# A hybrid attention block's first stage: scaling x in advance on POOL and DVE, both parts of u from ACT, weight loads on POOL's queue, fewer matrix-vector streams on TensorE

## The chip, the core and the metric

The kernel runs on one core of a Trainium2 chip. Its time is the device time of one execution in microseconds (us); a lower one is better. The engines are named as in the profile: PE (TensorE), DVE (VectorE), ACT (ScalarE), POOL (GpSimd) and SP (SyncE), which here only issues DMAs.

## The reference, cut to what matters

One decoder block over 512 tokens of width 2048, all in float32. The part that the first stage computes:

```
mod = silu(c) @ w_ada + b_ada                 # w_ada: 2048 x 12288; sections sh1, sc1, g1, sh2, sc2, g2
u   = rmsnorm(x, norm_attn) * (1 + sc1) + sh1
z   = u @ w_in                                # 2048 x 5664
...                                           # two kinds of attention on the columns of z, output product,
                                              # gated residual, SwiGLU, final RMSNorm
```

Of `mod`, only the sections sh1 and sc1 are needed for u: two matrix-vector products with 2048 x 2048 weights each.

## The kernel before, in words

**Layout.** Everything is kept transposed: a tile has 128 features on the partitions and the 512 tokens in a row. x is loaded by token and turned by PE into `xT` (16 tiles), and the row `rstd1` (1/rms of every token, the same on all partitions) comes from the sums of squares. A product in near float32 precision is made of three fp32r matmuls, for which each operand is split into a high part h (rounded by ACT) and a low part l (the rest, by DVE). So u is 16 pairs (h, l), and a `unit` is the three matmuls of one weight block with one u pair. Weights are loaded (`fetch_w`, tile `wr`), split by ACT into `wh` (L244) and by DVE into `wl` (L249).

**The first stage** is one loop over `step`, with its order written out by hand (`manual_schedule`): the instructions of each engine run in the order in which the loop emits them, and engines wait for each other by data alone. There are 8 rounds of 8 steps. Step n loads tile `ad` n: 256 rows of w_ada for 256 columns of sc1 and 256 of sh1, two DMAs on SP's queue (L509) into a ring of 8. A round is thus the mod values for two blocks of 128 features, and so for two tiles of u. In detail:

- One step after its load, DVE multiplies tile n by the entries of silu(c) and adds it to `acc` (L531, L533): a tile has two 128-row halves, one operation each. Where `on_pe(n)` is true, the second half is given to PE one step later, as a matmul with the broadcast column of silu(c) (L540, called a stream below), and gathered in a PSUM row that ACT copies out (`row`, L544).
- After the round's last tile, PE sums `row` and `acc` over the partitions by eight small matmuls each (L552); DVE adds the bias (`mod`, L560), forms `a_vec` = (1 + sc1) * norm_attn (L400), and `modulate_a` makes `mt` = xT * a_vec * rstd1 on DVE (L414) and h = round(mt + sh1) on ACT (L416). A step later `modulate_b` makes l = (mt + sh1) - h on DVE (L420).
- With two more tiles of u, units become possible. They wait in the list `todo` and are popped into PE's order at each step. Four PSUM banks `S0` gather the first half of the query product over u 0 to 7 (copied out by `keep_half`) and then the product `p_cmp` over all of u; three banks `S1` gather `p_s1` over all of u.
- `w_pairs(j)` asks for the weights of a round at step 8j+2 (round 0: at step 7) on SP's queue, in tiles shared by three or two buffers. In rounds 5 to 7 there are three of them, and the third is split at the round's fourth step, after the `modulate_a` of the third. Up to round 4 there are two, split at the round's first two steps.
- `tables()` builds the sine and cosine tables of the rotary embedding, one DVE operation a step, from step 14 on.

After the loop SP stores xT to DRAM (`xsp`, L590) behind the three weight loads of the next GEMM; memory of the stage is then used by the rotary steps (L609 to L616), which free the banks `S1` for that GEMM (second half of the query product).

Of the kernel before, what the change touches and what calls it, by code (L numbers as in the profile page):

```python
# [27 lines left out]
LAG = 2  # L28
LAGS = 2, 3, 4, 6
LAGS0 = 1, 2, 3, 0  # L30
KEEP = 12
R_C, R_D, R_F, R_V = 1.0, 1.0, 1.0, 0.6
SCALE = HD ** -0.5
NCMP = 31
# [45 lines left out]
def hymba_block(ctx: ExitStack, tc: tile.TileContext, x, c, positions, w_ada, b_ada, norm_attn,  # L80
# [21 lines left out]
    def uid(s):  # L102
        n_uid[0] += 1
        return f"{s}_{n_uid[0]}"
# [112 lines left out]
    def load_w(parts, ct, nk=2, extra=None, src=None, width=T, bufs=3):  # L217
        return fetch_w(parts, ct, nk, extra, src, width, bufs)()

    def fetch_w(parts, ct, nk=2, extra=None, src=None, width=T, bufs=3):  # L220
        pl = src or wts
        wr = pl.tile([P, nk, width], F32, tag="wr", name=uid("wr"), bufs=bufs)
        w = 0
        for part, n in parts:
            nc.sync.dma_start(wr[:, :, w:w + n], part(ct * nk * P, nk))
            w += n

        held = []

        def high():  # L230
            n_split[0] += 1
            if spare and n_split[0] % 3 == 0:
                both = spare[0].tile([P, 2, nk, width], F32R, tag="wx", name=uid("wx"), bufs=1)
                wh, wl = both[:, 0], both[:, 1]
            else:
                wh = pl.tile([P, nk, width], F32R, tag="wh", name=uid("wh"), bufs=2)
                wl = pl.tile([P, nk, width], F32R, tag="wl", name=uid("wl"), bufs=2)
            todo = [(slice(0, w), wr[:, :, 0:w])]
            if extra is not None:
                e = extra[:, ct * nk:(ct + 1) * nk, :]  # L240
                todo.append((slice(w, w + e.shape[2]), e))
            held.extend((wh, wl, todo))
            for sc, v in todo:
                nc.scalar.copy(wh[:, :, sc], v)  # L244
                if not early_high:
                    low(sc, v)

        def low(sc, v):
            nc.vector.tensor_tensor(held[1][:, :, sc], v, split_ap(held[0])[:, :, sc], op=OP.subtract)  # L249

        early_high = []

        def halves():
            if not held:
                high()
            else:
                for sc, v in held[2]:
                    low(sc, v)
            return held[0], held[1]

        def high_now():
            early_high.append(1)
            high()

        halves.high = high_now
        return halves
# [136 lines left out]
    def act_tile(name, i):  # L403
        h = act.tile([P, T], F32R, tag="ah", name=uid(name + "h"), bufs=ND)
        l = act.tile([P, T], F32R, tag="al", name=uid(name + "l"), bufs=ND)
        return h, l

    def modulate(which, i, src, rb, pl):
        return modulate_b(*modulate_a(which, i, src, rb, pl))

    def modulate_a(which, i, src, rb, pl):
        sh = mod[:, (0 if which == 0 else 3) * ND + i:(0 if which == 0 else 3) * ND + i + 1]
        t = pl.tile([P, T], F32, tag="mt", name=uid("mt"), bufs=2)
        nc.vector.scalar_tensor_tensor(t, src, a_vec[:, which, i:i + 1], rb, op0=OP.mult, op1=OP.mult)  # L414
        h, l = act_tile("u", i)
        nc.scalar.activation(h, t, AF.Identity, bias=sh)  # L416
        return h, l, t, sh

    def modulate_b(h, l, t, sh):
        nc.vector.scalar_tensor_tensor(l, t, sh, split_ap(h), op0=OP.add, op1=OP.subtract)  # L420
        return h, l

    cosT = sinT = None

# [32 lines left out]
    p_cmp = [cols(w_in, C_KC, 512)]  # L457
    p_s1 = [cols(w_in, C_KS, 256), cols(w_in, C_KW, 128)]
    part = None
    u = []  # L460
    NJ = ND // 2
    HJ = NJ // 2

    def w_pairs(j):
        s1 = fetch_w(p_s1, j, src=early, width=3 * P, bufs=2)
        if j < HJ:
            return [fetch_w(p_qn, j), s1]
        i = 2 * (j - HJ)
        return [fetch_w(p_cmp, i), s1, fetch_w(p_cmp, i + 1)]

    def unit(w, k, i, n, m, outs):
        return lambda: bank_pieces(("ws", m * P, P, outs[m]))[0](w[0], w[1], k, u[i], i == 0, i == n - 1)
# [21 lines left out]

    def on_pe(n):
        j, r = divmod(n, 8)
        return r < 7 if j == 0 else 2 <= r < (6 if j <= HJ else 4)

    tiles, accs, rows, sums, halves, fetched, todo = {}, {}, {}, {}, {}, {}, []
    extra_work = tables()  # L500
# [2 lines left out]
    while step < SLOTS + 8 or todo:  # L503
        j, r = divmod(step, 8)
        if j < NJ:
            tiles[step] = early.tile([P, 2, T], F32, tag="adw", name=uid("ad"), bufs=ADW)
            for i, sec in ((0, 1), (1, 0)):
                c0 = sec * D + j * 256
                nc.sync.dma_start(tiles[step][:, :, i * 256:(i + 1) * 256],  # L509
                                  w_ada[:, c0:c0 + 256].rearrange("(q p) n -> p q n", p=P)[:, 2 * r:2 * r + 2, :])  # L510
        if r == (2 if j else 7) and j < NJ:
            fetched[j] = w_pairs(j)
        if j == 1 and r < 2:
            fetched[0][r].high()
        i = AT.get(r, 3) if j < NJ else AT_END.get(r, 3)
        if 1 < j <= NJ and i < len(fetched[j - 1]):
            w = fetched[j - 1][i]()
            halves.setdefault(j - 1, []).append(w)
            pr = 2 * (j - 1 - HJ) + i // 2
            if j > HJ and i != 1:  # L520
                todo += units(w, pr, S0, ND)
        n = step - 1
        if 0 <= n < SLOTS:
            jj, q0 = n // 8, 2 * (n % 8)
            if q0 == 0:
                accs[jj] = early.tile([P, T], F32, tag="acc", name=uid("acc"), bufs=2)
            acc = accs[jj]
            for q in range(1 if on_pe(n) else 2):
                sc1 = sl[:, q0 + q:q0 + q + 1]
                if q0 + q == 0:  # L530
                    nc.vector.tensor_scalar(acc, tiles[n][:, q, :], sc1, None, op0=OP.mult)  # L531
                else:
                    nc.vector.scalar_tensor_tensor(acc, tiles[n][:, q, :], sc1, acc, op0=OP.mult, op1=OP.add)  # L533
        n = step - 2
        if 0 <= n < SLOTS and on_pe(n):
            jj, q = n // 8, 2 * (n % 8) + 1
            first = n == 0 or not on_pe(n - 1)
            if first:
                rows[jj] = bank("mm")
            nc.tensor.matmul(rows[jj], sl[:, q:q + 1].to_broadcast([P, P]), tiles[n][:, 1, :],  # L540
                             start=first, stop=not on_pe(n + 1))
            if not on_pe(n + 1):
                row = early.tile([1, T], F32, tag="row", name=uid("row"), bufs=2)
                nc.scalar.copy(row, rows[jj][0:1, :])  # L544
                rows[jj] = row
        n = due(step, 0)
        if n is not None:
            jj = n // 8
            sums[jj] = bank("mm")
            for av, one in ((rows.pop(jj), one_col[0:1, :]), (accs.pop(jj), one_col)):  # L550
                for i in range(4):
                    nc.tensor.matmul(sums[jj][:, i:i + 1], av[:, i * P:(i + 1) * P], one,  # L552
                                     start=one is not one_col and i == 0, stop=one is one_col,
                                     skip_group_check=True)
        n = due(step, 1)
        if n is not None:
            jj = n // 8
            for k2, sec in ((0, 1), (1, 0)):
                m0 = sec * ND + 2 * jj
                nc.vector.tensor_tensor(mod[:, m0:m0 + 2], sums[jj][:, 2 * k2:2 * k2 + 2], b_mod[:, m0:m0 + 2],  # L560
                                        op=OP.add)
            scale_vec(0, jj * 2, 2)
            pend = [modulate_a(0, i, xT[:, i, :], rstd1, early) for i in (2 * jj, 2 * jj + 1)]
            if jj == 0:
                halves[0] = [fetched[0][0]()]
        n = due(step, 2)
        if n is not None:
            u.extend([modulate_b(*h) for h in pend])
            jj = n // 8
            if jj == 0:  # L570
                halves[0].append(fetched[0][1]())
            if jj < HJ:
                todo += units(halves[jj][0], jj, S0, ND // 2) + units(halves[jj][1], jj, S1, ND)
            if jj == HJ - 1:
                todo.append(keep_half)
        n = due(step, 3 if step < SLOTS else 2)
        if n is not None and n // 8 >= HJ:
            todo += units(halves[n // 8][1], n // 8, S1, ND)
        for _ in range(3 if step >= 8 * HJ + LAGS[3] else 1 + (len(todo) > KEEP)):
            if todo:  # L580
                todo.pop(0)()
        if step >= 14:
            next(extra_work, None)
        step += 1
        if step == SLOTS + 6:
            z_first = [fetch_w(p_qn, HJ + i) for i in range(3)]
            w = z_first[0]()
            z_first[0] = lambda w=w: w
# [838 lines left out]
```

## Time and profile before

| | |
|---|---|
| median of 3 runs | 2457.55 us (2456.65 to 2460.13) |
| the profiled execution | 2450.92 us, of which the span of the trace is 2448.0 us |
| PE busy | 2355.1 us (96%) |
| PE weight loads busy | 2100.4 us (86%) |
| DVE busy | 1579.6 us (65%) |
| ACT busy | 1016.0 us (42%) |
| POOL busy | 341.5 us (14%) |
| mean granted clock of PE | 0.981 |

The span is the time from the first to the last instruction of one execution; windows are counted in us from its start. Busy times of different engines overlap. A granted clock of 1.00 is PE's higher level (2.4 GHz), 0.50 the lower one (1.2 GHz); a figure between them is a mean over a stretch that had both.

### The profile page before, as it was taken

To read this page: it belongs to the slowest core of one execution; us is meant where nothing else is said; L and a number is where in the kernel's file an instruction comes from. 1 tells how busy PE (TensorE), PEld (TensorE's weight loads), DVE (VectorE), ACT (ScalarE), POOL (GpSimd) and SP (SyncE) were. 2 spreads that over 40 slices of the span, in tenths; PEclk is the share of its full clock that TensorE was granted. 3 is DMA by queue.
4 is the path that set the end of the run, shared out by engine and by line. 5 is a ranking of instruction groups with operands and counts; after the bars stand their busy time and mean duration, and the time that the engine had idled before them with its cause. 6 is when DMAs were issued, how large, how long until landed. Compare 5 with 4: busy or idle time off the path is not lost.

```text
span 2448.0 us, 38482 instructions
## 1 busy us (share of the span) xinstructions
PE 2355.1 (96%) x14717; PEld 2100.4 (86%) x14717; DVE 1579.6 (65%) x2711; ACT 1016.0 (42%) x1531; POOL 341.5 (14%) x370
## 2 busy tenths in 40 slices
PE   6998999999999989889999999999999999999998
PEld 4677887888888767789999999999999888888887
DVE  6876786887755576596777777777776643333333
ACT  3224544344423332365555555555555422222133
POOL 0003002000001121251222121212221100000010
PEclk8998999999999999999999999999999999999999
DMA  9864743463554277559898989898988644333322
GB/s 332 283 198 147 205 139 95 130 190 117 180 174 129 85 249 253 186 122 237 211 231 215 228 213 232 220 225 212 221 200 193 192 151 141 123 120 121 102 95 101
DMA packets 322713, 440.31 MB, mean 180 GB/s; under 512 B 26224, under 2 KB 217552, under 8 KB 322528
## 3 DMA queue, kind: packets, MB, share of 16 engines
q1 hardware_dynamic: 289104, 348.21, 44.0%
q0 software_dynamic: 31120, 85.45, 18.7%
q10 hardware_dynamic: 2304, 4.20, 0.5%
q8 instruction: 115, 1.88, 0.3%
q14 instruction: 70, 0.57, 0.1%
HBM read 340.18 MB, written 28.38 MB: 151 GB/s over the span
## 4 chain that ended last, share of the span: by engine, by line
PE 54%; DVE 1%; DMA 0%; issue 0%; ACT 0%; SPq 0%; DVEq 0%; ACTq 0%
PE py L1161 12%; PE py L1164 11%; PE py L1163 11%; PE psmm L278 3%; PE psmm L279 3%; PE psmm L280 3%; PE pss L278 2%; PE pss L279 2%; PE pss L280 2%; PE pso L279 1%; PE pso L278 1%; PE pso L280 1%; DMA wr<-in_w_down_dram 0%; PE pso L1058 0%; DVE ul L1141 0%
## 5 line engine op out<-in xcount | busy, mean ns | idle before, releaser
L249 DVE TENSOR_TENSOR wl<-wr,wh 128x1024 fp32r<-128x1024 f32 (+2 forms) x211 | 239.0, 1133 | 381.5 <-ACT wh L244 378.4
L244 ACT CAST wh<-wr 128x1024 fp32r<-128x1024 f32 (+2 forms) x211 | 199.5, 948 | 502.7 <-PE psmm L279 199.7
L1164 PE MATMUL py<-uh,ls 128*128 128x256 f32 x1408 | 397.6, 282 | 3.6 <-DVE ls L1107 3.6
L1163 PE MATMUL py<-ul,hs 128*128 128x256 f32 x1408 | 397.6, 282 | 2.2 <-DVE ul L1141 2.2
L1161 PE MATMUL py<-uh,hs 128*128 128x256 f32 x1408 | 398.4, 283 | 1.0 <-DVE ev L1178 0.5
L1107 DVE TENSOR_TENSOR ls<-sum,hs 128x1024 fp32r<-128x1024 f32 x176 | 215.2, 1223 | 196.5 <-ACT hs L1101 196.5
L1101 ACT CAST hs<-sum 128x1024 fp32r<-128x1024 f32 x176 | 184.5, 1049 | 377.3 <-PE py L1163 257.5
L1163 PE MATMUL py<-ul,hx 128*128 128x256 f32 x1056 | 298.8, 283 | 4.0 <-DVE ul L1141 4.0
L1161 PE MATMUL py<-uh,hx 128*128 128x256 f32 x1056 | 299.3, 283 | 1.7 <-ACT uh L1140 1.4
L1164 PE MATMUL py<-uh,lx 128*128 128x256 f32 x1056 | 298.3, 282 | 0.0
L1164 PEld LDWEIGHTS py<-uh,ls 128*128 128x128 f32 x1408 | 267.0, 190 | 4.7 <-DVE ls L1107 4.6
L1163 PEld LDWEIGHTS py<-ul,hs 128*128 128x128 f32 x1408 | 267.0, 190 | 3.3 <-DVE ul L1141 3.3
L1161 PEld LDWEIGHTS py<-uh,hs 128*128 128x128 f32 x1408 | 267.1, 190 | 2.7 <-DVE ev L1178 1.3
L1097 POOL DMA_DIRECT2D lx<-raw x176 | 156.2, 887 | 580.2 <-ACT lx L1096 419.4
L1163 PEld LDWEIGHTS py<-ul,hx 128*128 128x128 f32 x1056 | 200.8, 190 | 5.1 <-DVE ul L1141 5.1
L1161 PEld LDWEIGHTS py<-uh,hx 128*128 128x128 f32 x1056 | 200.6, 190 | 2.2 <-ACT uh L1140 1.7
L1164 PEld LDWEIGHTS py<-uh,lx 128*128 128x128 f32 x1056 | 200.7, 190 | 0.0
L386 DVE SCALAR_TENSOR_TENSOR acc<-ad,sl,acc 128x512 f32<-128x512 f32 x180 | 141.6, 787 | 43.2 <-DMA ad<-in_w_ada_dram 41.4
L1092 ACT CAST hx<-raw 128x768 fp32r<-128x768 f32 x176 | 144.3, 820 | 11.3 <-DMA raw<-in_w_gate_dram 11.3
L1096 ACT ACTIVATE lx<-raw 128x768 fp32r<-128x768 f32 x176 | 148.1, 841 | 1.8 <-DMA raw<-in_w_gate_dram 1.8
L278 PE MATMUL psmm<-fh,wh 128*128 128x512 f32 x352 | 137.0, 389 | 0.0
L280 PE MATMUL psmm<-fh,wl 128*128 128x512 f32 x352 | 136.9, 389 | 0.0
(441 smaller groups left out, 5284.3 us busy)
## 6 DMA issues: line engine op xcount, KB each, us to landing
lx<-raw POOLq DMA_DIRECT2D x176, 384.0 KB, 5.2
ad<-in_w_ada_dram SPq DMA_DIRECT2D x128, 512.0 KB, 4.1
raw<-in_w_up_dram SPq DMA_DIRECT2D x176, 256.0 KB, 4.2
raw<-in_w_gate_dram SPq DMA_DIRECT2D x176, 256.0 KB, 4.5
wr<-in_w_down_dram SPq DMA_DIRECT2D x88, 512.0 KB, 3.6
ad<-in_w_ada_dram SPq DMA_DIRECT2D x128, 256.0 KB, 6.0
wr<-in_w_in_dram SPq DMA_DIRECT2D x104, 256.0 KB, 3.5
wr<-in_w_in_dram SPq DMA_DIRECT2D x24, 512.0 KB, 4.4
```

The source lines that it names most:

```text
L244: nc.scalar.copy(wh[:, :, sc], v)
L249: nc.vector.tensor_tensor(held[1][:, :, sc], v, split_ap(held[0])[:, :, sc], op=OP.subtract)
L278: nc.tensor.matmul(dst, wh[:, k, w], ah, start=first, stop=False)
L279: nc.tensor.matmul(dst, wh[:, k, w], al, start=False, stop=False)
L280: nc.tensor.matmul(dst, wl[:, k, w], ah, start=False, stop=last)
L1096: nc.scalar.activation(lx[s], raw[s][:, 1:4, :], AF.Copy, scale=-1.0)
L1097: nc.gpsimd.dma_start(split_ap(lx[s]), raw[s][:, 1:4, :], accum_op=OP.add)
L1101: nc.scalar.copy(hs[s], sums[s])
L1107: nc.vector.tensor_tensor(ls[s], sums[s], split_ap(hs[s]), op=OP.subtract)
L1161: nc.tensor.matmul(o, wh[:, wi, js], vh[:, vi, :], start=k == 0 and j == 0, stop=False, skip_group_check=True)
L1163: nc.tensor.matmul(o, wh[:, wi, js], vl[:, vi, :], start=False, stop=False, skip_group_check=True)
L1164: nc.tensor.matmul(o, wl[:, wi, js], vh[:, vi, :], start=False, stop=k == KG - 1, skip_group_check=True)
```

## The change

- x is scaled by rstd1 in advance: 16 products `xn` = xT * rstd1, two of them on DVE (steps 3 and 4) and 14 on POOL (from step 3 on, one a step in the emitted order). They lie in the 16 buffers that later take the low parts of u.
- ACT makes both h and t (the same value, not rounded) from xn with scale a_vec and bias sh1; the low part is one DVE subtraction, t - h. DVE's `mt` is gone.
- The weights of rounds 1 to 7 are asked for on POOL's queue.
- Streams: 5 in round 0 (7 before), 3 each in rounds 1 to 3 (4 before), none from round 4 on (4 in round 4, 2 each in 5 to 7 before). Where a round has none, the row and its eight small matmuls go.
- `todo` is popped by one rule: as many as are over 6, at least one, at most three. Before it was one a step, two if over 12 were waiting, and three from step 38 on.
- The tables start at step 3 instead of 14.

```
-KEEP = 12
+KEEP = 6
...
-    def fetch_w(parts, ct, nk=2, extra=None, src=None, width=T, bufs=3):
+    def fetch_w(parts, ct, nk=2, extra=None, src=None, width=T, bufs=3, eng=None):
...
-            nc.sync.dma_start(wr[:, :, w:w + n], part(ct * nk * P, nk))
+            (eng or nc.sync).dma_start(wr[:, :, w:w + n], part(ct * nk * P, nk))
...
-        t = pl.tile([P, T], F32, tag="mt", name=uid("mt"), bufs=2)
-        nc.vector.scalar_tensor_tensor(t, src, a_vec[:, which, i:i + 1], rb, op0=OP.mult, op1=OP.mult)
-        h, l = act_tile("u", i)
-        nc.scalar.activation(h, t, AF.Identity, bias=sh)
-        return h, l, t, sh
-
-    def modulate_b(h, l, t, sh):
-        nc.vector.scalar_tensor_tensor(l, t, sh, split_ap(h), op0=OP.add, op1=OP.subtract)
-        return h, l
+    u = []
+    xn = [act.tile([P, T], F32, tag="al", name=f"xn{i}", bufs=ND) for i in range(ND)]
+
+    def norm_x(i, eng):
+        eng.tensor_tensor(xn[i], xT[:, i, :], rstd1, op=OP.mult)
+
+    def modulate(i):
+        h = act.tile([P, T], F32R, tag="ah", name=uid("uh"), bufs=ND)
+        t = early.tile([P, T], F32, tag="mt", name=uid("mt"), bufs=2)
+        for dst in (h, t):
+            nc.scalar.activation(dst, xn[i], AF.Identity, scale=a_vec[:, 0, i:i + 1], bias=mod[:, i:i + 1])
+        return h, t
+
+    def modulate_low(h, t):
+        l = act.tile([P, T], F32R, tag="al", name=uid("ul"), bufs=ND)
+        nc.vector.tensor_tensor(l, t, split_ap(h), op=OP.subtract)
+        u.append((h, l))
...
     def w_pairs(j):
-        s1 = fetch_w(p_s1, j, src=early, width=3 * P, bufs=2)
+        eng = nc.gpsimd if j else nc.sync
+        s1 = fetch_w(p_s1, j, src=early, width=3 * P, bufs=2, eng=eng)
...
-        return r < 7 if j == 0 else 2 <= r < (6 if j <= HJ else 4)
+        return r < 5 if j == 0 else j < HJ and 2 <= r < 5
...
-            pend = [modulate_a(0, i, xT[:, i, :], rstd1, early) for i in (2 * jj, 2 * jj + 1)]
+            pend = [modulate(i) for i in (2 * jj, 2 * jj + 1)]
...
-            u.extend([modulate_b(*h) for h in pend])
+            for p in pend:
+                modulate_low(*p)
...
-        for _ in range(3 if step >= 8 * HJ + LAGS[3] else 1 + (len(todo) > KEEP)):
+        for _ in range(max(1, min(3, len(todo) - KEEP))):
             if todo:
                 todo.pop(0)()
-        if step >= 14:
+        if step >= 3:
+            if step < 5:
+                norm_x(step - 3, nc.vector)
+            if step < 17:
+                norm_x(step - 1, nc.gpsimd)
             next(extra_work, None)
```

## Rows read from the trace of the kernel before

**Rows 1.** Rounds: length; busy PE, PEld, DVE, ACT, POOL; PEclk, DMA share, GB/s.

```profile
22.38:34.45 12.07, 8.84 (x22) 4.58 (x22) 6.50 (x10) 2.14 (x4) 0.00 (x0) 0.86 1.10 351
34.45:57.05 22.60, 16.20 (x65) 11.48 (x66) 16.57 (x26) 4.85 (x7) 0.00 (x0) 0.77 1.08 344
57.05:74.04 16.99, 14.79 (x58) 10.71 (x59) 16.81 (x31) 3.64 (x5) 0.00 (x0) 0.90 0.99 313
74.04:91.82 17.78, 16.44 (x64) 12.03 (x64) 16.65 (x30) 6.07 (x8) 0.00 (x0) 0.88 0.97 314
91.82:111.04 19.22, 19.22 (x69) 13.88 (x68) 13.49 (x22) 3.64 (x5) 0.00 (x0) 0.84 0.66 202
111.04:130.89 19.85, 18.19 (x78) 13.77 (x79) 17.43 (x28) 5.66 (x8) 0.00 (x0) 1.00 0.89 285
130.89:149.82 18.93, 18.93 (x87) 14.90 (x86) 16.31 (x25) 4.69 (x6) 0.00 (x0) 1.00 0.95 299
149.82:168.92 19.10, 19.10 (x88) 15.05 (x87) 15.37 (x25) 4.58 (x6) 0.00 (x0) 1.00 0.56 181
sum 146.54, PE 131.71 PEld 96.41 DVE 119.14 ACT 35.27 POOL 0.00; mean PE 16.46 PEld 12.05 DVE 14.89 ACT 4.41 POOL 0.00
```

**Rows 2.** Instructions of PE in order of time: start us, us, what.

```profile
61.33 1.02 PE L540 MATMUL psmm<-ad,sl 128*128 128x512 f32 x2
...
62.89 0.40 PE L278 MATMUL psmm<-uh,wh 128*128 128x512 f32 x1
...
172.59 1.05 PE L552 MATMUL psmm<-cs,row 1*128 1x1 f32 x8
173.57 1.05 PE L552 MATMUL psmm<-cs,acc 128*128 128x1 f32 x8
174.48 0.48 PE L278 MATMUL psmm<-uh,wh 128*128 128x512 f32 x1
...
191.10 0.39 PE L278 MATMUL psmm<-uh,wh 128*128 128x512 f32 x1
```

**Rows 3.** Instructions of DVE in order of time, idle time before them in brackets.

```profile
61.74 0.69 DVE L443 SCALAR_TENSOR_TENSOR sinT<-kk,posi 128x512 f32<-128x512 f32 x1
...
72.83 0.42 DVE L437 TENSOR_SCALAR kk<-kk 128x512 f32<-128x512 f32 x1
...
134.31 1.42 DVE L414 SCALAR_TENSOR_TENSOR mt<-xT,a_vec,rstd 128x512 f32<-128x512 f32 x2
137.46 1.22 DVE L249 TENSOR_TENSOR wl<-wr,wh 128x1024 fp32r<-128x1024 f32 x1 [1.73 <-ACT wh L244]
...
167.47 1.53 DVE L533 SCALAR_TENSOR_TENSOR acc<-ad,sl,acc 128x512 f32<-128x512 f32 x2
```

**Rows 4.** Instructions of ACT in order of time.

```profile
24.42 0.59 ACT L177 COPY rstd<-psmm 128x512 f32<-128x512 f32 x1 [2.83 <-PE psmm L175]
...
135.10 1.39 ACT L416 ACTIVATE uh<-mt,mod 128x512 fp32r<-128x512 f32 x2 [6.97 <-DVE mt L414]
136.39 1.03 ACT L244 CAST wh<-wr 128x1024 fp32r<-128x1024 f32 x1
...
194.63 0.59 ACT L609 ACTIVATE sw<-psmm 64x512 f32<-64x512 f32 x1 [2.50 <-DMA xsp<-xT]
```

**Rows 5.** DVE in a later stretch, before and beside products on POOL.

```profile
785.74 0.69 DVE L249 TENSOR_TENSOR wl<-wr,wh 128x512 fp32r<-128x512 f32 x1 [2.06 <-ACT wh L244]
...
791.81 1.46 DVE L951 SCALAR_TENSOR_TENSOR yl<-or,vec,yh 128x512 fp32r<-128x512 f32 x1 [0.25 <-ACT yh L950]
```

**Rows 6.** POOL in order of time: one product alone, then eight beside DVE.

```profile
195.91 1.27 POOL L612 TENSOR_TENSOR sw<-sw,sinT 128x512 f32<-128x512 f32 x1 [189.83 <-ACT sw L610]
...
786.76 12.67 POOL L948 TENSOR_TENSOR or<-or,rbn 128x512 f32<-128x512 f32 x8 [19.32 <-ACT rbn L177]
```

**Rows 7.** Waits of SP's queue, 0 to 200 us: total us, times, longest.

```profile
SPq L225 <- DVE wl L249: 42.8, 6, 11.4
```

**Rows 8.** Costliest groups of the page: busy us, mean ns; idle before.

```profile
L1097 POOL DMA_DIRECT2D lx<-raw x176 | 156.2, 887 | 580.2 <-ACT lx L1096 419.4
```

More of the change, by code (lines that the diff above doesn't have):

```diff
@@ L406, in act_tile @@
         return h, l
[L408 to L412, printed above, removed]
-        t = pl.tile([P, T], F32, tag="mt", name=uid("mt"), bufs=2)
-        nc.vector.scalar_tensor_tensor(t, src, a_vec[:, which, i:i + 1], rb, op0=OP.mult, op1=OP.mult)
-        h, l = act_tile("u", i)
-        nc.scalar.activation(h, t, AF.Identity, bias=sh)
-        return h, l, t, sh
-    def modulate_b(h, l, t, sh):
-        nc.vector.scalar_tensor_tensor(l, t, sh, split_ap(h), op0=OP.add, op1=OP.subtract)
-        return h, l
+    u = []
[12 more added lines that the diff above has]
+        u.append((h, l))
     cosT = sinT = None
@@ L459, in hymba_block @@
     part = None
-    u = []
     NJ = ND // 2
@@ L464, in w_pairs @@
     def w_pairs(j):
-        s1 = fetch_w(p_s1, j, src=early, width=3 * P, bufs=2)
+        eng = nc.gpsimd if j else nc.sync
+        s1 = fetch_w(p_s1, j, src=early, width=3 * P, bufs=2, eng=eng)
         if j < HJ:
-            return [fetch_w(p_qn, j), s1]
+            return [fetch_w(p_qn, j, eng=eng), s1]
         i = 2 * (j - HJ)
-        return [fetch_w(p_cmp, i), s1, fetch_w(p_cmp, i + 1)]
+        return [fetch_w(p_cmp, i, eng=eng), s1, fetch_w(p_cmp, i + 1, eng=eng)]
     def unit(w, k, i, n, m, outs):
@@ L549, in hymba_block @@
             sums[jj] = bank("mm")
-            for av, one in ((rows.pop(jj), one_col[0:1, :]), (accs.pop(jj), one_col)):
+            srcs = ([(rows.pop(jj), one_col[0:1, :])] if jj in rows else []) + [(accs.pop(jj), one_col)]
+            for av, one in srcs:
                 for i in range(4):
                     nc.tensor.matmul(sums[jj][:, i:i + 1], av[:, i * P:(i + 1) * P], one,
-                                     start=one is not one_col and i == 0, stop=one is one_col,
+                                     start=i == 0 and one is srcs[0][1], stop=one is one_col,
                                      skip_group_check=True)
```

## The prediction

> **What bounds the kernel now.** Only the first stage is edited, so I read only that stage, and three rows from elsewhere that price what it lacks. First the table of the stage by rounds [rows 1]: a round is the eight steps that bring one pair of 128-row blocks of u, cut here where VectorE starts the next round's sum. The eight rounds take 146.54 us (22.38 to 168.92). The reader is to see which column is full in which round. In rounds 0 and 1 it is the DMA share (1.10, 1.08, near 350 GB/s). In rounds 2 and 3 it is DVE (16.81 of 16.99, 16.65 of 17.78), with DMA close behind. In rounds 4, 6 and 7 TensorE has no gap at all, and DVE idles 5.73, 2.62 and 3.73 us. So no engine alone bounds the stage: three are within some 15% of each other, and an edit that frees one gains only down to the next.
>
> Next, the order in time on PE [rows 2]. The last round's sums stand at 172.59 although DVE's last addition began at 167.47 [rows 3]: PE was 3.7 us behind. From the end of these sums (174.48) to the first product of the next GEMM (191.10) PE runs 16.6 us without a gap. That start, and ScalarE's first rope step at 194.63, which waited for the xsp stores [rows 4], are where the stage hands on. What moves them moves the end; from there on nothing is edited, so I carry the shift to the end unchanged.
>
> **TensorE's part.** A stream is one fp32 matmul in two passes. From its start at 61.33 to the second unit at 62.89 a stream and a unit take 1.56 us [rows 2]. A unit is three matmuls; 24 of them fill the 16.6 us, so 0.69 us each. A stream therefore costs 0.87. Before there are 7 + 4x4 + 3x2 = 29, after 5 + 3x3 = 14: 15 fewer, 13.0 us. Rounds 4 to 7 have no row any more, so four times its eight small matmuls go, 0.98 us each (172.59 to 173.57): 3.9 us. PE loses 16.9 us of 131.7. If PE bound the stage this would be the gain.
>
> **VectorE's part.** The 15 streams come back as multiply-adds of 0.77 (two in 1.53, [rows 3]): +11.5 us. Sixteen products mt at about 0.71 go (two in 1.42): -11.4. The low half becomes a subtraction, at 0.69 [rows 5] against about 0.7: nothing. Two products xn stay on DVE: +1.4. So DVE's work is about the same, 119 + 2 us. What changes is its waits, in three places.
>
> *First, POOL's 14 products.* POOL's queue is not held to the steps; they need only xT and rstd1, which is written at 24.42 + 0.59 = 25.0 [rows 4]. So they run back to back from there, in front of the additions of round 0. The trace before has no POOL arithmetic in this stage, so the price is from the nearest rows. Alone such a product takes 1.27 us; eight independent ones beside a working DVE took 12.67, 1.58 each [rows 6], and DVE's two-input operations between them took 1.46 instead of 0.7 to 0.77 [rows 5]. The engines take turns, one for one. DVE loses between 0.7 (1.46 less 0.77) and 1.27 (a whole product) for each, 10 to 18 us in all; the lower end is about 5 if DVE idles under them as it does now (5.57 us idle in round 0). I take 0.95, nearest the eight in a row: 13.3 us.
>
> The Trainium skill (SBUF — State Buffer, Who interferes with whom) says that a DVE instruction with two SBUF inputs and a GpSimd instruction that reads SBUF exclude each other for the whole of the one that started first; at 1.27 for each product that would be 17.8 us, and the sum below would come out 4.5 us later. The trace agrees on the turns; it shows less than the whole as the loss.
>
> *Second, the tables.* They start at step 3 instead of 14. Of the 18 DVE operations, 0.69 or 0.42 each [rows 3], pitched 0.6 and 0.35, five now stand in round 0 (2.1 us), eight in round 1 instead of two (+3.0), five in round 2 instead of eight (-1.3), none in round 3 (-3.4).
>
> *Third, ScalarE now makes h and t, four operations instead of two* (1.39 for two, 0.65 apart, [rows 4]). Before, mt began at 134.31 and covered most of it: the split of the round's third weight tile started at 137.46 after a wait of 1.73 [rows 3], because its ACT half stands behind both uh. After, DVE has nothing between a_vec and that split: 0.05 + 4x0.65 + 1.03 + 0.05 = 3.7 us empty, against 3.2 from mt to the split now, 1.4 of it work. Behind it on DVE wait the additions of the next steps, hence the whole round. It applies in rounds 5 to 7, which have a third weight tile; in 2 to 4 about 1 us of waiting for t replaces mt.
>
> **Queues.** SP waited 42.8 us, in six waits, for weight buffers [rows 7], with w_ada loads queued behind; on POOL's queue these waits hold only later weight loads. Worth something where DVE waits for data, which it hardly does after round 0. Each such issue takes POOL about 0.89 [rows 8], three or four in a round; those of round 1 stand behind seven products, so at about 37 us, and are needed at 67. Free. The three loads for z and xsp stay on SP and wait as before for the last split. KEEP and the popping rule leave PE six units in hand instead of about five to ten; I take nothing.
>
> **The sum.**
> - Round 0, additions done: 25.0, plus 15 DVE operations left (8 multiply-adds, 2 products, 5 of the tables) 9.5, plus 12 turns of 0.95, 11.4: 45.9, where round 1 starts at 34.45 now.
> - Round 1: busy 16.57 + 0.77 - 1.5 + 3.0 + two turns 1.9 = 20.8 (22.60 now): 66.7.
> - Round 2: 16.81 + 0.77 - 1.5 - 1.3 + 1.0 = 15.8: 82.5.
> - Round 3: 16.65 + 0.77 - 1.5 - 3.4 + 1.3 = 13.8, but its 5.1 MB (16 loads of 256 KB and two of w_in) need 14.6 at 350 GB/s: 97.1.
> - Round 4: 13.49 + 3.1 - 1.5 + 0.6 = 15.7, its 5.6 MB need 16.1: 113.2.
> - Round 5: 19.85 + 1.54 + 0.5 - 0.1 = 21.8: 135.0. Round 6: 18.93 + 1.95 = 20.9: 155.9. Round 7: 19.10 + 1.95, less PE's lag 1.6 and the earlier wait: about 19.9 to the last addition: 175.8, against 168.9 now.
>
> DVE is then 6.9 us later. PE gives back the 3.7 us that it is late and the row's 0.98: the sums end at 176.8 instead of 174.48, +2.3. Behind them come about as many units as now, 25 by the new rule. But PE, with 16.4 us of work in rounds of 21 (22 units and one sum), now stands idle before each sum, and the granted clock fell to 0.77 and 0.90 in the rounds where it did so [rows 1]; at the lower level for some us, the tail costs about 2 more. The third split, and xsp behind it, come 2.9 us later (2.3 plus ACT's two extra operations, less mt). So the stage ends 3 to 6 us later; I take 5. On the profiled execution (2448.0 span, 2450.92 in all) that is 2456; on the median of the three runs, which lies 6.6 above it, 2462.5.
>
> **Rivals.**
> *PE's saving comes out.* POOL's products cost DVE little, and rounds 4 to 7 fall to what PE and DMA need (16.1 to 18 instead of 19). For it: PE's unbroken rounds. Against: DVE's waits above. It takes 6 to 17 us off: 2440 to 2452, near 2447. It decides if a POOL product costs DVE under about 0.3 us.
> *The two cancel.* With turns of 0.5 us (7 us instead of 13.3) DVE's end lies at about 169.5 and PE's sums at 170.5: minus 4 to plus 4, 2454 to 2462. For it: the low end of the bound.
> *PE's clock.* If the pauses keep PE at the lower level for most of rounds 5 to 7, 22 units at up to 1.3 us do not fit into 21 us, and the end comes 11 to 20 us later: 2469 to 2477. For it: rounds 1 and 3 at 0.77 and 0.88. Against: those had shorter rounds of pauses and recovered within them.
> *Weights late on POOL's queue* would show in DVE waiting for them; with 30 us of margin in round 1 and a round in the later ones I give it nothing of its own.
>
> **Numbers.** A change under 0.2% (4.9 us) is about what can't be told from none. Forecast, 0 to 11 us slower (2458 to 2469): 0.50. The two cancel: 0.17. PE's saving: 0.23. PE's clock: 0.10. Of the forecast's half, 0.35 lies above 4.9 us; so slower 0.45, the same 0.30, faster 0.25. The range 2445 to 2472 leaves out the best third of PE's saving and most of the clock case.
>
> **What would show it.** POOL's 14 products from 25 to about 48, 1.6 to 1.7 us apart, and DVE additions of 1.4 and more between them; round 1 starting near 46; four ACT operations in a row in each round and DVE empty 3.7 us before the third split; PE with gaps before its sums in rounds 5 to 7; last sums near 176, next GEMM near 195. I am wrong if round 1 starts before 40, if rounds 5 to 7 stay under 19.5 us, or if PE still has no gap there.

## The result, and the profile after

The change made the kernel slower: 2477.23 us (median; 2473.02 to 2479.97) against 2457.1 before, a ratio of 1.0084 [1.0059, 1.0109], some 20 us. The forecast was 2462.5 with a range up to 2472. The side was right; the size was not.

The stage again by rounds, cut as in [rows 1], for the kernel after:

```profile
22.85:49.33 26.48, 8.36 (x29) 5.25 (x29) 25.50 (x20) 3.46 (x5) 19.63 (x15) 0.63 0.88 279
49.33:72.81 23.48, 16.83 (x67) 12.54 (x68) 20.27 (x31) 5.19 (x7) 5.04 (x5) 0.77 0.71 222
72.81:94.40 21.59, 16.51 (x59) 11.20 (x57) 14.59 (x26) 7.73 (x10) 2.16 (x3) 0.76 0.75 238
94.40:113.63 19.23, 17.61 (x67) 12.81 (x66) 12.90 (x21) 5.18 (x7) 2.88 (x4) 0.83 0.92 294
113.63:130.11 16.48, 13.94 (x57) 10.45 (x58) 15.07 (x25) 5.78 (x8) 2.88 (x4) 0.90 1.00 309
130.11:151.71 21.60, 16.96 (x70) 13.10 (x70) 17.21 (x28) 5.64 (x7) 2.88 (x4) 0.92 0.82 261
151.71:172.24 20.53, 17.75 (x76) 14.37 (x76) 16.10 (x25) 5.66 (x7) 2.88 (x4) 0.92 0.86 275
172.24:191.91 19.67, 17.12 (x70) 13.68 (x69) 15.24 (x25) 5.66 (x7) 0.00 (x0) 0.91 0.28 87
```

Read it column by column against [rows 1]. Round 0 is more than twice as long, and DVE is busy in nearly all of it. In rounds 2 and 3 no column is full any more: DVE is busy 14.59 of 21.59 and 12.90 of 19.23, PE 16.51 and 17.61, and DMA moves 238 and 294 GB/s where it reached 350. A round that no engine fills is a chain of waits. Only round 4 is shorter than before. In rounds 5 to 7 PE has gaps, where in rounds 6 and 7 it had none.

How the stage is measured below: from the start of round 0 to ScalarE's first rope step, 22.85 to 213.17 = 190.32 us, against 194.63 - 22.38 = 172.25 before. That is 18.1 us more (17.2 against the second profile of before). The rest of the span is 2474.2 - 213.17 = 2261.0. In the profile shown of before it is 2253.4, so the span differs by 26; in a second profile of the unedited kernel (below) it is 2260.7, and in the traces of the experiments 2257.9 to 2264.5. The change therefore left the rest as it was.

Round 0 itself began between 22.4 and 26.6 us over the traces of this case, and lengths are counted from there. A good part of this difference goes with the queue edit. In five of the experiments (no products, all products on DVE, the queue alone, and the two with all three repairs) POOL has no products to make, and its queue sends off the weight loads of round 1 between 7 and 11 us, beside the loads of x. These five begin round 0 at 25.7 to 26.6, the other nine traces at 22.4 to 25.0. In the kernel after, the same loads stand behind seven products, at 36.88. They are 0.9 MB, which is 2.6 us at 350 GB/s (an estimate). No run holds the loads back, so the cause is read from comparing traces and is not tested. A stage length of these five leaves out some 3 us that they pay before it; for them the place of the rope step is given too.

POOL after the change, in order of time; the number in brackets is idle time before, and what ended it:

```profile
25.77 11.16 POOL L412 TENSOR_TENSOR xn<-xT,rstd 128x512 f32<-128x512 f32 x7 [19.68 <-ACT rstd L177]
36.88 2.21 POOL L225 DMA_DIRECT2D wr<-in_w_in_dram  x3
39.10 6.32 POOL L412 TENSOR_TENSOR xn<-xT,rstd 128x512 f32<-128x512 f32 x5
52.76 2.97 POOL L412 TENSOR_TENSOR xn<-xT,rstd 128x512 f32<-128x512 f32 x2 [7.33 <-ACT mt L418]
```

And DVE in the same stretch:

```profile
27.77 1.78 DVE L536 SCALAR_TENSOR_TENSOR acc<-ad,sl,acc 128x512 f32<-128x512 f32 x1
...
39.07 5.24 DVE L442 TENSOR_SCALAR kk<-kk 128x512 f32<-128x512 f32 x1
44.23 2.53 DVE L536 SCALAR_TENSOR_TENSOR acc<-ad,sl,acc 128x512 f32<-128x512 f32 x2
...
52.79 3.48 DVE L536 SCALAR_TENSOR_TENSOR acc<-ad,sl,acc 128x512 f32<-128x512 f32 x2
```

Twelve products run from 25.77 to 45.4 beside round 0's additions, as forecast; an addition beside one takes 1.7 to 1.8 us instead of 0.77. Now the end of a later round, where POOL makes no products. First ACT, then DVE, then PE, round 2:

```profile
89.38 0.57 ACT L547 COPY row<-psmm 1x512 f32<-1x512 f32 x1 [7.17 <-PE psmm L543]
89.86 1.78 ACT L244 CAST wh<-wr 128x1024 fp32r<-128x1024 f32 x2
```

```profile
90.94 1.23 DVE L249 TENSOR_TENSOR wl<-wr,wh 128x1024 fp32r<-128x1024 f32 x1 [5.58 <-ACT wh L244]
```

```profile
77.36 0.80 PE L278 MATMUL pss<-uh,wh 128*128 128x512 f32 x1 [3.12 <-ACT uh L418]
...
88.33 1.02 PE L543 MATMUL psmm<-ad,sl 128*128 128x512 f32 x2
```

This is the wait that the prediction does not have. DVE is empty for 5.58 us until ACT has made the high half of a weight tile. ACT could have made it earlier: with the split put first (below), it makes it 6.5 us after the round's start, not 17. But here the copy of the row stands ahead of the split in ACT's order, and it waited 7.17 us for PE's last stream. PE came to that only at 88.33, because units stood in front of the streams and between them; the first of these need the pair of u that ACT was just making, and PE stood idle for them for 3.12 us. The releaser named on DVE's row is ACT; the cause is one engine further back, on PE. The same wait is 2.85 us in round 1 and 4.25 in round 3. Last, ACT and DVE in round 5:

```profile
134.38 0.81 ACT L418 ACTIVATE uh<-xn,mod,a_vec 128x512 fp32r<-128x512 f32 x1 [9.76 <-DVE a_vec L400]
135.10 0.80 ACT L418 ACTIVATE mt<-xn,mod,a_vec 128x512 f32<-128x512 f32 x1
135.81 0.80 ACT L418 ACTIVATE uh<-xn,mod,a_vec 128x512 fp32r<-128x512 f32 x1
136.51 0.80 ACT L418 ACTIVATE mt<-xn,mod,a_vec 128x512 f32<-128x512 f32 x1
137.22 2.80 ACT L244 CAST wh<-wr 128x1024 fp32r<-128x1024 f32 x3
```

```profile
138.28 1.23 DVE L249 TENSOR_TENSOR wl<-wr,wh 128x1024 fp32r<-128x1024 f32 x1 [4.00 <-ACT wh L244]
```

That one was forecast (at 3.7 us): four operations in a row on ACT, DVE empty 4.00 us behind them, in each of rounds 5 to 7.

### The profile page after: what moved, and what is told of

The parts are those of the page before. It is cut to its first block, busy times and chain, and to the rows that moved or that the text cites. A ratio compares the mean times of both kernels' runs of the same rounds, so it can differ in the third digit from the quotient of the medians.

```text
span 2474.2 us, 38399 instructions
## 1 busy us (share of the span) xinstructions
PE 2351.4 (95%) x14655; PEld 2099.7 (85%) x14655; DVE 1598.2 (65%) x2712; ACT 1027.2 (42%) x1543; POOL 380.8 (15%) x409
## 4 chain that ended last, share of the span: by engine, by line
PE 54%; DVE 1%; DMA 0%; issue 0%; ACT 0%; DVEq 0%; SPq 0%; ACTq 0%
PE py L1170 11%; PE py L1173 11%; PE py L1172 11%; PE psmm L280 3%; PE psmm L278 3%; PE psmm L279 3%; PE pss L278 2%; PE pss L279 2%; PE pss L280 2%; PE pso L280 1%; PE pso L279 1%; PE pso L278 1%; DMA wr<-in_w_down_dram 0%; PE pso L1067 0%; PE psmm L1403 0%
```

## The experiments

After each edit: the length of the stage (190.32 in the kernel after, 172.25 and 173.12 in the two profiles of before), then the time and its ratio to before. The theory at the start: the 20 us are the products on POOL, the row's copy ahead of the split, and the third split behind ACT's four operations, and the rest of the change moves little. Its rivals stand in the expectations.

**No products.** This kernel leaves out the scaling by the token's norm and so the products on both engines.

```diff
-            nc.scalar.activation(dst, xn[i], AF.Identity, scale=a_vec[:, 0, i:i + 1], bias=mod[:, i:i + 1])
+            nc.scalar.activation(dst, xT[:, i, :], AF.Identity, scale=a_vec[:, 0, i:i + 1], bias=mod[:, i:i + 1])
...
-            if step < 5:
-                norm_x(step - 3, nc.vector)
-            if step < 17:
-                norm_x(step - 1, nc.gpsimd)
```

> The changed kernel without the 16 products xT * rstd1: ACT reads xT itself, so u (and all that follows) is not scaled by the token's norm; nothing else is edited. Theory (POOL's 14 products and DVE's two-input operations exclude each other, in turns): round 1 starts near 36 us instead of 49.3, and the end of the stage, read as ScalarE's first rope step, comes 14 to 16 us earlier than 213.2, at 197 to 199; the time is about 2462. Rival (round 0 is long because of the two additions that came back from TensorE and the tables that start earlier): round 1 still starts after 43 and the rope step after 207; time above 2470.

Measured: 173.96 us, 16.4 shorter (rope step at 199.96, 13.2 earlier); 2461.56 us, 1.0014 [1.0004, 1.0024]. Its rounds 0 and 1:

```profile
26.00:37.67 11.67, 8.50 (x29) 5.30 (x29) 10.17 (x18) 3.46 (x5) 0.00 (x0) 0.79 1.10 351
37.67:59.20 21.53, 16.83 (x67) 12.54 (x68) 18.21 (x32) 5.19 (x7) 2.20 (x3) 0.80 1.04 337
```

Round 0 loses 14.8 us and round 1 2.0; DMA is full again in round 0. Round 1 starts at 37.67 and the rope step comes 1 us later than expected, as round 0 began 3.2 us later; the rival is out. Take off DVE's own two products at about 0.6, and a product on POOL cost 15.2/14 = 1.1 us. The later rounds stayed as long as after: another part of the loss lies there.

**All products on DVE.**

```diff
-            if step < 5:
+            if step < 19:
                 norm_x(step - 3, nc.vector)
-            if step < 17:
-                norm_x(step - 1, nc.gpsimd)
```

> The changed kernel with all 16 products on VectorE, one a step from step 3, none on POOL. Theory (a product on POOL costs VectorE a whole turn, over 1 us while it is full, and one of its own costs it 0.6): rounds 0 and 1 together take about 41 us instead of 50 although VectorE does 14 more operations, and the rope step comes at 203 to 207 instead of 213.2. Rival (what the engines lose to each other is small beside the operation's own time): rounds 0 and 1 take 50 us or more, the rope step 213 to 220.

Measured: 178.81 us, 11.5 shorter than with 14 of them on POOL (rope step at 205.33, 7.8 earlier, as expected; rounds 0 and 1 take 37.9, less than expected); 2465.93 us, 1.0034 [1.0013, 1.0055]. Its rounds 0 and 1:

```profile
26.52:41.29 14.77, 9.05 (x31) 5.91 (x32) 13.78 (x25) 3.46 (x5) 0.00 (x0) 0.73 1.08 348
41.29:64.42 23.13, 16.79 (x66) 12.36 (x66) 22.95 (x39) 5.19 (x7) 2.13 (x3) 0.80 0.86 263
```

Six products stand in round 0 and make it 3.1 us longer than none; from the start of one to the next operation a product takes 0.6, and half a us falls into a wait that is there without them. So a product cost DVE less when DVE made it than when POOL did, 0.6 against 1.1, and all sixteen together cost the stage only 4.85 (178.81 - 173.96), since in the later rounds they fall into DVE's waits.

**The old popping rule.**

```diff
-KEEP = 6
+KEEP = 12
...
-        for _ in range(max(1, min(3, len(todo) - KEEP))):
+        for _ in range(3 if step >= 8 * HJ + LAGS[3] else 1 + (len(todo) > KEEP)):
```

> The changed kernel with the popping rule of before (one unit a step, two if over 12 wait, three from step 38). Theory (up to three units a step stand in front of the streams in TensorE's order, so the row comes late, and the weight split stands behind the row's copy on ScalarE): VectorE's waits for the first split of rounds 1, 2 and 3 (2.9, 5.6 and 4.3 us) fall under 1.5 each and the rope step comes at 203 to 206 instead of 213.2. Rival (the row is late because u comes late and TensorE is then at the lower clock, whatever the rule): at least two of the waits stay above 3.5 us and the rope step comes at 209 to 214.

Measured: 179.56 us, 10.8 shorter; 2464.79 us, 1.0024 [1.0014, 1.0034]. Rounds 2 and 3:

```profile
71.49:87.42 15.93, 13.33 (x51) 9.68 (x49) 14.50 (x26) 7.74 (x10) 2.16 (x3) 0.84 1.04 339
87.42:103.84 16.42, 16.42 (x66) 12.51 (x65) 12.90 (x21) 5.19 (x7) 2.88 (x4) 0.84 1.00 323
```

DVE's wait for the first split falls to 0.60, nothing and 1.44 us, and the rope step comes at 203.66: the theory held. The new rule lets up to three units go in one step, and they stand in front of the streams that the row waits for. This rule, for which the prediction put down nothing, is most of what rounds 1 to 3 lost (10.7 us of the 13.1 by which they passed the forecast).

**The split ahead of the row's copy.** The first two splits of a round are asked of ACT before the row is copied.

```diff
+        if 1 <= j < HJ and r == 5:
+            fetched[j][0].high()
+            fetched[j][1].high()
```

> The changed kernel with ScalarE's halves of the first two weight splits of rounds 1 to 3 emitted at the round's sixth step, before the row's copy. Theory (ScalarE's order alone makes VectorE wait): the waits of 2.9, 5.6 and 4.3 us go, rounds 2 and 3 take 16.5 us or less (21.6 and 19.2 now), and the rope step comes at 200 to 203. Rival (TensorE is behind, and the wait only moves to the sums): VectorE waits 3 us or more for the sums in rounds 2 and 3 instead, and the rope step comes at 208 to 213.

Measured: 177.53 us, 12.8 shorter; 2464.81 us, 1.0025 [1.0015, 1.0034]. Rounds 1 to 3:

```profile
49.24:69.77 20.53, 15.14 (x50) 10.80 (x50) 20.18 (x31) 5.17 (x7) 5.01 (x5) 0.71 0.63 189
69.77:85.69 15.92, 13.82 (x61) 10.07 (x61) 14.50 (x25) 7.62 (x10) 2.16 (x3) 1.00 1.04 338
85.69:100.59 14.90, 14.90 (x61) 11.15 (x60) 12.81 (x22) 5.18 (x7) 2.88 (x4) 0.89 1.06 353
```

The rope step comes at 200.72, as the theory had it. Only the order on ACT is changed here, PE's is not; the three waits are gone, and these rounds fall to what DVE, then DMA, then PE and DMA need.

**The third split ahead of ACT's four operations.**

```diff
             scale_vec(0, jj * 2, 2)
+            if jj >= HJ:
+                fetched[jj][2].high()
             pend = [modulate(i) for i in (2 * jj, 2 * jj + 1)]
```

> The changed kernel with ScalarE's half of the third weight split emitted before the four operations that make h and t, in the rounds that have a third tile. Theory (VectorE stands empty 4.0 us a round behind these four): the wait falls under 1 us, rounds 5 to 7 take 18.5 us or less (21.6, 20.5 and 19.7 now), and the rope step comes at 203 to 207. Rival (rounds 5 to 7 are held by TensorE's work or the transfers at 19 to 20 us): the rounds shorten by less than 1 us each and the rope step comes after 210.

Measured: 180.81 us, 9.5 shorter; 2464.92 us, 1.0033 [1.0022, 1.0044]. Rounds 5 and 6:

```profile
131.29:148.84 17.55, 14.94 (x69) 12.17 (x68) 17.16 (x27) 5.67 (x7) 2.89 (x4) 0.97 0.98 323
148.84:165.31 16.47, 16.47 (x64) 13.64 (x65) 16.05 (x26) 4.91 (x7) 2.89 (x4) 0.82 1.05 340
```

DVE's busy time is as it was (16.05 against 16.10 in round 6); 4 us of waiting are gone in each round, 12.0 in the three. The stage gains 9.5 of them: PE is 1.8 us further behind at the last sums, and rounds 0 to 3, which this edit does not touch, took 0.7 us more in this trace. Single rounds of theirs differ by up to 1.4 us between the two traces, so a difference of that size in one round shows nothing.

**All three** (split before row, third split first, products on DVE), the three diffs together.

> The changed kernel with three repairs at once: all products on VectorE, the splits of rounds 1 to 3 ahead of the row's copy, the third split ahead of the four operations. Theory (the three waits are separate and add up until TensorE or the transfers bound the stage): rounds of about 15, 22, 18, 15, 17, 17.5, 16.5 and 17 us, the rope step at 184 to 190, the time 2447 to 2453, below before. Rival (one cause behind all three, TensorE's lower clock with its late start, so that one repair does the work of all): rope step at 197 to 203, time above 2458.

Measured: 158.20 us (rope step at 183.91), 2447.3 us, 0.9964 [0.995, 0.9977], faster than before and as expected. The three alone shorten the stage by 33.8 in sum, together by 32.1; counted by the rope step, 29.3 and 29.3. So the three are separate losses. The last round is full on PE:

```profile
146.53:163.00 16.47, 16.47 (x78) 13.69 (x77) 16.05 (x25) 5.78 (x7) 0.00 (x0) 1.00 0.39 124
```

**All three and the old popping rule.**

> The kernel with the three repairs, and the popping rule of before as well. Theory (once the weight splits stand ahead of the row's copy, it does not matter how many units stand ahead of the streams): round 0 to rope step, 158.2 us with the new rule, stays within 3 us, the time within 4 us of 2447. Rival (the units themselves hold up TensorE's sums and with them every round): 5 us or more shorter.

Measured: 158.58 us (rope step at 184.59), 2445.6 us, 0.9947 [0.9931, 0.9964], as the theory had it. With the row's wait gone the rule has nothing left to cost: 0.4 us in the stage.

**The tables from step 14, as before.**

```diff
-            next(extra_work, None)
+            if step >= 14:
+                next(extra_work, None)
```

> The changed kernel with the sine and cosine tables from step 14 on, as before. Theory (in rounds 0 and 1 each of the early operations takes a turn with POOL, in rounds 2 and 3 the same operations would fill time in which VectorE waits for the weight split): rounds 0 and 1 together take 41 to 45 us instead of 50, rounds 2 and 3 at most 2 us more than 40.8, and the rope step comes 4 to 8 us earlier than 213.2. Rival (the same work in another place, as the sum had it): rope step at 211 to 215.

Measured: 188.68 us (rope step at 213.65), 2475.02 us, 1.0072 [1.0057, 1.0087]. The theory, 4 to 8 us earlier, fell, and the rival held. Rounds 0 and 1 become shorter together (47.0 instead of 50.0), rounds 2 and 3 longer (42.2 instead of 40.8): the same work in another place. Part of why shows on DVE:

```profile
65.99 0.49 DVE L434 TENSOR_SCALAR posi<-posi,cs 128x512 f32<-128x512 f32 x1 [6.45 <-ACT posi L433]
```

The cast of the positions now stands behind the row's copy on ACT and waits with it.

**The queue alone, on the kernel before.**

```diff
-            nc.sync.dma_start(wr[:, :, w:w + n], part(ct * nk * P, nk))
+            (eng or nc.sync).dma_start(wr[:, :, w:w + n], part(ct * nk * P, nk))
...
+        eng = nc.gpsimd if j else nc.sync
...
```

> The kernel before with one part of the change: the weights of rounds 1 to 7 asked for on POOL's queue. Theory (VectorE hardly waits for data after round 0, so SP's waits for weight buffers cost nothing): the rope step within 3 us of 194.6 and the time within 4 us of before. Rival (w_ada loads held behind weight loads set the pace): SP's loads run ahead, rounds 1 to 7 shorten, rope step before 190, time 5 us or more below.

Measured: 170.92 us in the stage, 1 to 2 shorter than before (rope step at 197.52, 1 to 3 later); 2462.26 us, 1.0015 [1.0002, 1.0029]. The time is 4 to 6 us up (3.7 by the ratio, 5.8 by the medians), at the edge of what was expected or outside it, though the stage is not longer. The trace shows where 1 to 3 of them can come from. POOL has nothing else to do and sends round 1's weights off at once:

```profile
7.64 0.73 POOL L225 DMA_DIRECT2D wr<-in_w_in_dram  x1 [1.53 <-DMA rows<-in_norm_attn_dram]
8.95 1.43 POOL L225 DMA_DIRECT2D wr<-in_w_in_dram  x2 [0.58 <-DMA rows<-in_norm_ffn_dram]
```

DMA is full there already (364 GB/s from 5 to 10 us, 355 before), and round 0 begins at 26.6 instead of 22.4 and 23.5. What is left of the 4 to 6 us is not accounted for.

**Fewer streams alone, on the kernel before.**

```diff
-        return r < 7 if j == 0 else 2 <= r < (6 if j <= HJ else 4)
+        return r < 5 if j == 0 else j < HJ and 2 <= r < 5
...
-            for av, one in ((rows.pop(jj), one_col[0:1, :]), (accs.pop(jj), one_col)):
+            srcs = ([(rows.pop(jj), one_col[0:1, :])] if jj in rows else []) + [(accs.pop(jj), one_col)]
+            for av, one in srcs:
...
```

> The kernel before with one part of the change: 14 streams on TensorE instead of 29, the other halves added on VectorE, no row from round 4 on. Theory (VectorE is as full as TensorE in these rounds, and it gets 11.5 us more work): the rope step comes 0 to 6 us later than 194.6, the time 0 to 6 us above before. Rival (TensorE bounds the stage, the 16.9 us taken from it come out): rope step before 188, time 6 us or more below.

Measured: 167.37 us, 2450.35 us, 0.9977 [0.9968, 0.9986]. Neither expectation held: it is about 5 us shorter, not longer, and not by as much as the rival had it. Of the 4.9 us (172.25 less 167.37) only 0.9 come before the last addition; 3.7 come between it and the last sums, because PE is less far behind and the row's eight matmuls are gone. DVE's wait for the last sums, in the kernel before and here:

```profile
174.66 0.23 DVE L560 TENSOR_TENSOR mod<-psmm,vec 128x2 f32<-128x2 f32 x2 [4.79 <-PE psmm L552]
```

```profile
171.34 0.23 DVE L561 TENSOR_TENSOR mod<-psmm,vec 128x2 f32<-128x2 f32 x2 [1.04 <-PE psmm L553]
```

The rounds show the wait behind the row again, which the kernel before has too. ACT, and DVE, of the kernel before in round 4:

```profile
106.03 0.58 ACT L544 COPY row<-psmm 1x512 f32<-1x512 f32 x1 [8.89 <-PE psmm L540]
```

```profile
107.58 1.23 DVE L249 TENSOR_TENSOR wl<-wr,wh 128x1024 fp32r<-128x1024 f32 x1 [5.41 <-ACT wh L244]
```

Without a row in round 4 there is no such wait, and the round takes 16.88 instead of 19.22, though DVE has more to do. Rounds 5 and 6 give most of it back (21.02 instead of 19.85, and 19.83 instead of 18.93). Rounds 4 and 5:

```profile
92.67:109.55 16.88, 12.82 (x58) 10.34 (x58) 16.42 (x26) 3.16 (x4) 0.00 (x0) 0.98 0.85 265
109.55:130.57 21.02, 19.98 (x80) 16.20 (x80) 18.84 (x30) 5.08 (x7) 0.00 (x0) 0.85 0.84 268
```

**Fewer streams and the third split first, on the kernel before**: the last diff with the two lines of the third split. Nothing is put on POOL.

> The kernel before with 14 streams, and ScalarE's half of the third weight split emitted before the operations that make h (two in this kernel). Theory (the wait of 1.7 us in rounds 5 to 7 goes): round 0 to rope step, 167.4 us without this edit, takes 163 to 165; the time is 2445 to 2449. Rival (TensorE holds these rounds): 166 to 168, time 2449 to 2452.

Measured: 161.13 us, 2444.4 us, 0.9943 [0.9928, 0.9958], a little beyond what was expected. The wait of 1.7 us is gone, and rounds 5 and 6 are 1.8 us shorter each than with fewer streams alone. It is the fastest of the medians, but its interval overlaps those of both kernels with all three repairs. The rope step comes at 183.77, within 0.8 us of theirs: their stage is shorter and begins 3 us later. Rounds 5 and 6:

```profile
108.48:127.69 19.21, 19.21 (x78) 15.84 (x78) 18.75 (x29) 5.41 (x8) 0.00 (x0) 0.86 0.92 293
127.69:145.70 18.01, 17.98 (x85) 14.68 (x85) 17.55 (x27) 5.03 (x6) 0.00 (x0) 1.00 0.99 315
```

**The kernel before, unedited, a second time.**

> The kernel before once more, unedited, for a second trace. Theory (the 7.7 us by which the rest of the changed kernel, from the rope step to the end, was longer in the first two traces are the spread between executions): round 0 to rope step within 1 us of 172.3, the rest between 2257 and 2264 us instead of 2253.4. Rival (the change costs time behind the first stage too): the rest again below 2255.

Measured: 173.12 us in the stage, and 2457.4 - 196.66 = 2260.7 for the rest, where the first profile had 2253.4. ACT's first rope step:

```profile
196.66 0.59 ACT L609 ACTIVATE sw<-psmm 64x512 f32<-64x512 f32 x1 [2.47 <-DMA xsp<-xT]
```

So the 7.6 us by which the rest seemed longer after the change are a difference between executions.

## Why the prediction was wrong in size, step by step

**The step that failed** is the sum of rounds 1 to 3. "Round 2: 16.81 + 0.77 - 1.5 - 1.3 + 1.0 = 15.8" starts from DVE's busy time, and so do its neighbours, as if every wait in these rounds had gone with the work. And of KEEP and the popping rule it says "I take nothing". Predicted were 20.8, 15.8 and 14.6; measured 23.48, 21.59 and 19.23, 13.1 us more. That is the wait behind the row's copy, 2.85, 5.58 and 4.25 us by itself. With the split ahead of the row the rounds were 20.53, 15.92 and 14.90, what the prediction said: the work was priced rightly, and the wait was not seen. Most of it comes from the units that the new rule puts in front of the streams (the stage is 10.8 us shorter with the old rule, 12.8 with the split first). The wait could be seen in the trace before, in round 4 (above) and in round 1, where it is a good part of the 6 us by which DVE's busy time falls short of the round (the row below). In rounds 2 and 3 of that trace it was nothing and 0.45 us: there it is new after the change.

```profile
53.26 1.23 DVE L249 TENSOR_TENSOR wl<-wr,wh 128x1024 fp32r<-128x1024 f32 x1 [4.86 <-ACT wh L244]
```

Round 4's sum drops its wait of 5.41 us as well and came out, 16.1 against 16.48. There the row is gone and the wait with it, but the sum does not say so: in this respect it was luck. None of the three signs of being wrong came either; none of them looks at rounds 1 to 3.

**A term that was too small** is the turns with POOL: 12 of 0.95 in round 0, which was to last to 45.9 and lasted to 49.33. Of these 3.4 us, 0.7 are rstd1, written at 25.7 instead of 25.0 (0.5 of it the later start of the round), and 0.6 are a table operation: six stand in round 0, where the sum counted five. That leaves 2.1 for the turns, 13.5 in all instead of 11.4, 1.1 for a product. The two turns in round 1 cost 1.95, as forecast.

For all fourteen that is 15.5; the experiment gives 15.2 (16.4 without any products, less 1.2 for DVE's own two), 1.9 more than the 13.3 from the rows. The rule of the Trainium skill (SBUF — State Buffer, Who interferes with whom), a whole product of DVE's time for each, gave 17.8 us for the fourteen; the 15.2 lie about halfway between it and the 13.3.

**Right:** the third split, 3.7 predicted, 4.00 measured, and rounds 4 to 7 with it: 16.1, 21.8, 20.9, 19.9 predicted; 16.48, 21.60, 20.53, 19.67 measured. The tables, which only change rounds. The weight loads of round 1 on POOL's queue, which went out at 36.88, behind seven products; that the same edit can send them off beside the loads of x, where POOL has no products, was not seen. The 4.7 us that PE was to give back at the last sums: it gave back 4.5. PE's pauses ahead of the sums, 4.12 in round 5 and 2.77 in the last round:

```profile
151.07 1.02 PE L556 MATMUL psmm<-cs,acc 128*128 128x1 f32 x8 [4.12 <-DVE acc L536]
...
192.14 1.02 PE L556 MATMUL psmm<-cs,acc 128*128 128x1 f32 x8 [2.77 <-DVE acc L536]
...
193.48 0.63 PE L279 MATMUL psmm<-ul,wh 128*128 128x512 f32 x1
...
197.23 0.40 PE L280 MATMUL pss<-uh,wl 128*128 128x512 f32 x1
```

After the last of them PE's matmuls took 0.63 instead of 0.40 us up to 196.5, about 2 us in all, as the sum had it. The rival of PE's clock did not happen: the granted clock of rounds 5 to 7 is 0.92, 0.92 and 0.91, and their length is DVE's wait, as the third split's experiment shows.

**The account.** The last addition was to end at 175.8 and ended at 191.9. Of the 16.1 us, 13.1 are rounds 1 to 3, 3.0 round 0, 0.5 its start, and rounds 4 to 7 gave back 0.4. The rope step came 18.5 us later than before instead of 5; 2.3 us of the shift were taken up by the xsp stores, for which it now waits 0.23 instead of 2.50. That the change would be slower was forecast for two of the three causes, the turns and the third split; the wait behind the row, which it did not see, is most of what made it 20 us instead of 5. Part of PE's saving is there: fewer streams alone are 0.9977, with the third split first 0.9943. What lost is the products on POOL, the units ahead of the row's streams, and the third split behind ACT's two further operations.

## What to carry to other kernels

When a round's length is worked out from an engine's busy time, ask of every wait in the old round whether the edit removes its cause, and carry it over if not; where the edit changes the order in a queue, ask also which waits are new. A wait on ScalarE may have its cause two engines back: look at what stands ahead of the instruction in its queue, and at what that waits for. Work moved from a full VectorE to GpSimd is not off VectorE if it comes in a block beside it: here a product cost VectorE 1.1 us on GpSimd and 0.6 on VectorE itself. A load moved to a queue that has nothing else to do leaves as early as its buffer allows: look at what it then runs beside.

## What the runs showed of the hardware that was not expected

- DVE and POOL did not always take turns one for one. Two-input additions beside POOL's products took 1.7 to 1.8 us; one-input operations took 1.5 instead of 0.42 to 0.48, and the one at 39.07 took 5.24 us while POOL made its next five products in 6.32 us, at the pace that it has alone (1.26 each). Whether DVE had to wait for all of the five can't be read from one row.
- An ACT operation over 128x512 with a scale and a bias for each row took 0.80 us (0.71 apart), the one with a bias alone about 0.69 (0.65 apart, [rows 4]); four of them make the third split's 4.00 instead of 3.7.
- POOL's last two products began at 52.76, after 7.33 us, when ACT's first t was done, which they neither read nor overwrite (at 50.67, again behind the first t, with the tables from step 14). They fell on additions of round 1 (3.48 us for two). Why they waited was not tried.
